# Ends of two mixers moved between the input projections, and RWKV's 32x32 products spread over the array

## The chip, the cores and the metric

The kernel runs on one core of a Trainium2 chip. Its time is the device time of one execution in microseconds; the median of three runs is given. A core has a matrix engine (TensorE, PE in the profile; its weight loads are PEld), a vector engine (VectorE, DVE), a scalar engine (ScalarE, ACT), a general one (GpSimd, POOL) and a queue from which all transfers here are issued (SyncE, SP). Each engine works through its own instructions in their order and waits on semaphores for the others. Products are made by PE into PSUM banks of 128 partitions by 512 fp32 elements.

## The reference

The kernel is a trunk of two layers over 512 latent and 256 context tokens of width 1024. Each layer is an FFN, a mixing of tokens by four groups of heads side by side, and another FFN. The mixing makes one input projection, runs GLA, a Mamba-2 (ssm), RWKV-7 and attention on its columns, puts their outputs side by side and applies one output projection:

```
ux = modulate(x, p['norm_g'][1], mx[3], mx[4]) @ p['w_in']
gla_c, gla_x = gla_mixer(...); ssm_c, ssm_x = mamba_mixer(...)
rw_c, rw_x = rwkv_mixer(...);  at_c, at_x = attention_mixer(...)
x = x + mx[5] * (concatenate([gla_x, ssm_x, rw_x, at_x]) @ p['w_out'])
```

Two of these groups have an end that needs only their own columns. That of ssm: `y = y + d_skip * xs`, times `silu(z)`, then an RMS norm over 256 columns. That of GLA: an RMS norm of each head's 64 columns, times `silu(g)`. RWKV is a recurrence over tokens, in both directions; the kernel does it in chunks of 64 tokens, for which it needs the inverse of a triangular 64x64 matrix for each head and chunk.

## The kernel before, in words

Activations lie with channels on the partitions and tokens along the free axis (768 tokens in layer 0, of which 256 are context; in layer 1 the context is needed only as a source, so many products have 512). Large products are made of three fp32r products of high and low parts (`split`, line 78, makes them: ACT rounds to the high part, DVE or POOL subtracts for the low one).

`mix` is the mixing stage. It makes the input projection in 25 tiles of 128 columns, most of them through `proj`, which loads two weight pieces, splits them and runs 24 groups of products into one of two PSUM tiles; the operand of all of them is h, eight high and eight low tiles. Between the projections stand the parts of the mixers that need them. Toward the end of `mix` come the two triangular inverses of RWKV (`x_rwkv_inverse`, lines 1410 and 1412, 31 steps of two DVE operations for each direction, its result stored in DRAM as `td` and `pd`), the gates sz0, sz1, gg1, gg0 (stored in DRAM by `spill`), the projection lg, four of attention (ak, qA, qB, av; `x_att_in`), and four of RWKV (v0, v1, r0, r1; `x_rwkv_in`, an ACT copy with scale and four DVE operations that shift by a token, lines 1221 to 1230). Only then follow

- `x_ssm_end`: multiply F by the gate z (line 1195), square on ACT, add on POOL (1202), sum over the partitions by products with a column of ones (`group_stats`), an inverse root in some dozen tiny DVE operations (`rsqrt`, lines 94 to 100), a spread of the roots back over the partitions (`spread`: ACT copy at line 838, transposes on PE at line 843), and a DVE operation that applies them (1210);
- `x_gla_end`: the same for the two tiles of GLA (lines 985 to 996);
- the fetch of gates gg1 and gg0 and their product with GLA's tiles (1843);
- `y_parts`: the high and low parts of the four tiles, written into tiles `hl0` to `hl3` and `hh4` to `hh7`, that is into the places of h.

Then `open_second` gives the rooms of the projections (SBUF and PSUM) to the second half of the stage: `rwkv`, the part of the output projection that needs GLA and ssm alone (`x_out`, PE tile `sc`, DVE line 1783, weights through one buffer `wa`), and attention (`x_att`).

`rwkv` goes through a list, `SCHEDULE`, of units (U), solves (S), steps (T) and outputs (Y); a unit is four chunks of one direction, so there are six units and six solves in each layer. `x_rwkv_unit` starts with the load of the decays (`dec`) and builds the matrices `A0`; its first products are `pr<-R,B`. `x_rwkv_solve` assembles the inverse of each 64x64 matrix from two inverted 32x32 diagonal blocks and their coupling: it loads the blocks (`PY<-pd`, `A<-td`), makes 16 products of 32x32 into one PSUM bank (`pr<-PY,A`), copies them, makes 16 more (`pr<-A,PY`) and copies these into the coupling block of `A0`. All 16 of a group read one strip of 32 partitions and write one strip of 32. `WT`, the result of the solve, has three buffers.

Program order is not engine order. The kernel is built with a planner (`schedule_with_timeline_sim=True` in the last function) that puts each engine's instructions in order ahead of time from its own estimate of durations; of what it holds for ready, the first in program order goes first. So an operation may run before others that stand ahead of it in the text. Waits and buffers follow from the tiles: a tile's place is given on when its last reader is done.

Of the kernel before, what the change touches and what calls it, by code (L numbers as in the profile page):

```python
# [12 lines left out]
ALU = mybir.AluOpType  # L13
# [39 lines left out]
class Net:  # L53
# [1363 lines left out]
    def x_rwkv_solve(self, d, b, unit, td, pd):  # L1417
        nc, rw = self.nc, self.rw
        A0, A1, ZV, ZU, R = unit
        cs = slice(4 * b, 4 * b + 4)  # L1420
        r1 = slice(64 + 32 * d, 96 + 32 * d)
        r2 = slice(96 - 32 * d, 128 - 32 * d)
        c2 = slice(32 - 32 * d, 64 - 32 * d)
        A = A0.rearrange("p h e c t -> p (h e) c t")
        P1 = rw("PY", (512,))
        for q in range(4):
            self.load(P1[r1].rearrange("p (q c t) -> p q c t", q=4, c=4)[:, q], pd[q // 2, q % 2, cs].rearrange("c s t -> s c t"))
            for i in range(2):
                self.load(A[64 + 32 * i:96 + 32 * i, q, :, 32 * i:32 * i + 32], td[i, q // 2, q % 2, cs].rearrange("c s t -> s c t"))
        py, px = self.bank(), self.bank()  # L1430
        each = [(q, c, slice(32 * (4 * q + c), 32 * (4 * q + c) + 32)) for q in range(4) for c in range(4)]
        for q, c, u in each:
            self.mm(py[r2, u], A[r1, q, c, c2], P1[r1, u])
        self.copy(P1[r2], py[r2])
        for q, c, u in each:
            self.mm(px[r1, u], P1[r2, u], A[r2, q, c, c2])
        self.copy(A.rearrange("p q c t -> p (q c) t")[r1, :, c2], px[r1].rearrange("p (q t) -> p q t", t=32))
        pw = self.bank()
        for hp in range(2):
            for c in range(4):  # L1440
                for e in range(2):
                    u = 64 * (4 * hp + c)
                    self.mm(pw[64 * e:64 * e + 64, u:u + 64], ZU[:, hp, c, e], A0[:, hp, e, c])
        WT = rw(f"WT{self.nR % self.UNITS[1]}", (2, 4, 64))
        nc.vector.tensor_copy(WT.rearrange("p h c t -> p (h c t)"), pw)
        self.heads_apart(self.bank(), lambda hp, c, e: (A0[64:128, hp, e, c], ZV[64:128, hp, c, e]), ZV)
        return WT

# [10 lines left out]

    def x_rwkv_step(self, d, n, unit, WT, PC, H, Hn):  # L1460

        nc = self.nc
        A0, A1, ZV, ZU, R = unit
        c = n % 4
        pc = self.bank("pc")
        pv = pc.rearrange("p (h x) -> p h x", h=2)
        halves = [slice(0, 64), slice(64, 128)]
        if H is not None:
            Hd = self.rw("Hd", (2, 64))
            nc.gpsimd.tensor_tensor(Hd, H, PC[:, :, n:n + 1].to_broadcast([128, 2, 64]), op=ALU.mult)  # L1470

            for hp in range(2):
                for es in halves:
                    self.mm(pv[es, hp, 0:64], WT[es, hp, c], H[es, hp])
            for e, es in enumerate(halves):
                z = ZV[64:128, :, c, e]
                nc.vector.tensor_tensor(z, pv[es, :, 0:64], z, op=ALU.add)
        for hp in range(2):
            for e, es in enumerate(halves):
                self.mm(pv[es, hp, 128:192], A1[:, hp, c, e, 1], ZV[:, hp, c, e])  # L1480
        if H is not None:
            nc.vector.tensor_tensor(Hn, Hd, pv[:, :, 128:192], op=ALU.add)
        else:
            nc.vector.tensor_copy(Hn, pv[:, :, 128:192])
        return Hn
# [42 lines left out]
    def rwkv(self, l, U, T, PC, ld, ya, need_ctx):  # L1528
# [5 lines left out]
        H = [[None], [None]]  # L1534
        unit, WT = {}, {}
        seen = set()
# [5 lines left out]
        def solve(d, s):  # L1542
            unit[d, s] = unit[d]
            WT[d, s] = self.x_rwkv_solve(d, parts[d][s], unit[d], *T[d])
        def step(d, i):
            n = self.chunks(d)[i]
            if i < 5:
                Hs[d].append(self.rw(f"H{d}{i}", (2, 64)))
            H[d].append(self.x_rwkv_step(d, n, unit[d, i // 4], WT[d, i // 4], PC[d], H[d][-1], Hs[d][i % 5]))
# [244 lines left out]
    def mix(self, l, h, need_ctx, early):  # L1794
        nc = self.nc
        nt = NT if need_ctx else NX
        self.ud = {}
        y = {}
        self.open_mix()
        self.x_rwkv_consts(l)  # L1800
        self.open_first()
        names = self.FIRST
        kp, kk, bb = [self.pair(n) for n in ("k", "kk", "bb")]
        wa = self.room("wa")
        for n, us, p in zip(names, (wa, kp[:, 0], kp[:, 1]), self.first_projs(l, names, h)):
            self.x_rwkv_in(l, n, h, NT, us, p)
        self.wa = wa
        nc.scalar.activation(out=wa[0:64], in_=wa[0:64], func=AF.Tanh)
        misc = self.x_misc(l, h)
        self.x_rwkv_prep(l, kp, kk, bb)  # L1810
        dts = self.x_ssm_dt(l, misc)
        T, PC, ld, nd = self.rwkv_inverses(l, (kk, bb))
        gqk = self.pair("gqk")
        G = [gqk[:, 0], gqk[:, 1], misc]
        self.x_gla_in(l, h, nt, G)
        self.qd, self.kn = self.pair("qd"), self.pair("kn")
        D = [self.x_gla_dir(l, d, G, nt) for d in range(2)]
        F = self.x_ssm_in(l, h, nt)
        gqk = self.pair("gqk")
        yg = [gqk[:, i] for i in range(2)]  # L1820
        for b in (2, 0, 1) if need_ctx else (0, 1):
            self.x_gla_block(l, b, D, yg)
        self.x_ssm(l, F, dts, need_ctx)
        self.x_rwkv_inverse(0, nd[0], *T[0])
        self.x_rwkv_inverse(1, nd[1], *T[1])
        for name in ("sz0", "sz1", "gg1", "gg0"):
            self.gate(l, name, h, nt)
        sg = self.x_rwkv_in(l, "lg", h, nt, self.stage())
        self.sigmoid_from(sg[:, :nt], sg[:, :nt])
        self.spill(l, "lg", sg, nt)  # L1830
        rope = self.x_att_rope()
        for name in ("ak", "qA", "qB", "av"):
            self.x_att_in(l, name, h, NT if name[0] == "a" else nt, rope)
        v, r = self.pair("kn"), self.pair("qd")
        for t, n, w in ((v, "v", NT), (r, "r", nt)):
            for hp in range(2):
                self.x_rwkv_in(l, f"{n}{hp}", h, w, t[:, hp])
        z = [self.fetch(f"sz{i}", self.gt(f"xT{i}"), nt) for i in range(2)]
        self.x_ssm_end(l, F, z, nt)
        self.x_gla_end(l, yg, nt)  # L1840
        for i in (1, 0):
            g = self.fetch(f"gg{i}", self.gt("misc"), nt)
            nc.vector.tensor_tensor(yg[i][:, :nt], g[:, :nt], yg[i][:, :nt], op=ALU.mult)
        for i in (1, 0):
            self.y_parts(y, i, yg[i], nt)
        for i in range(2):
            self.y_parts(y, 2 + i, F[i], nt)
        self.open_second()
        ya = self.hp.tile([128, 2, NT], F32, tag="hl45", name="y45")
        y[4], y[5] = ya[:, 0], ya[:, 1]  # L1850
        self.rwkv(l, (r, kp, v, kk, bb), T, PC, ld, ya, need_ctx)
        self.x_out(l, y, nt)
        self.left.close()
        self.right.close()
        self.base.close()
        self.open_early(early)
        self.x_att(l, y, need_ctx)
        self.outer.close()
        return y
# [171 lines left out]
```

## Time and profile before

| | us |
|---|---|
| median of three runs | 3250.92 |
| lowest and highest | 3242.71, 3254.85 |
| the profiled execution | 3241.78 |
| its span, first to last instruction | 3240.0 |
| PE busy | 3042.4 (94%) |
| DVE busy | 2464.2 (76%) |
| ACT busy | 1254.9 (39%) |
| POOL busy | 912.8 (28%) |

Matmuls overlap and their ends are modelled, so a busy PE is not one at its peak. The mean granted clock of PE over the span is 0.956 of full speed; it has two levels, 2.4 and 1.2 GHz. The chain that ended last is followed back from the last instruction, at each step to what released it.

### The profile page before, as it was taken

Reading aid. Unit: us, or ns where it says so; the run is one execution under the profiler, and the core shown is the slowest. Engines: PE = TensorE matmul, PEld = TensorE weight load, DVE = VectorE, ACT = ScalarE, POOL = GpSimd, SP = SyncE. Lnnn points to the kernel's source line nnn. Section 1 sums busy time; section 2 is a strip of 40 time slices with the busy share of each in tenths; the row PEclk is TensorE's granted clock in tenths of the full one; section 3 lists DMA queues with packets and bytes.
Section 4 is the critical chain, followed back from the end, with each engine's and each line's share of the span. In section 5 each row is a group of like instructions: output and inputs, shape, how many; then the busy total and the mean of one; then the engine's idle time right before and its main releaser. Section 6 shows DMA issues by size and latency. Waiting matters only on the chain.

```text
span 3240.0 us, 55398 instructions
## 1 busy us (share of the span) xinstructions
PE 3042.4 (94%) x21340; PEld 2690.3 (83%) x21340; DVE 2464.2 (76%) x4669; ACT 1254.9 (39%) x2256; POOL 912.8 (28%) x712
## 2 busy tenths in 40 slices
PE   6999999898979988999999999999898879989999
PEld 3899999777868757999998899999776767679899
DVE  7999899567854458788888787888657855487878
ACT  3333334343234444333334333333443235454444
POOL 0143333144232100233330132324145332004433
PEclk9999999898889999999999999999998879999999
DMA  6344343223224022333343233332324132133233
GB/s 253 100 132 146 124 138 117 98 73 87 77 86 120 12 95 86 101 123 118 118 130 98 72 123 105 111 120 95 115 64 120 61 93 68 43 108 101 89 102 124
DMA packets 184344, 335.79 MB, mean 104 GB/s; under 512 B 64752, under 2 KB 80976, under 8 KB 183696
## 3 DMA queue, kind: packets, MB, share of 16 engines
q1 hardware_dynamic: 184080, 332.25, 32.2%
q8 instruction: 168, 2.75, 0.4%
q14 instruction: 96, 0.79, 0.1%
HBM read 304.99 MB, written 27.18 MB: 103 GB/s over the span
## 4 chain that ended last, share of the span: by engine, by line
PE 77%; DVE 13%; DMA 5%; issue 2%; ACT 2%; SPq 1%; POOL 0%; DVEq 0%; ACTq 0%; POOLq 0%
PE pt L63 57%; PE pj L63 6%; PE pr L63 4%; PE sc L63 3%; DVE wlo L78 2%; PE pg L63 1%; DVE inv L1412 1%; DVE T L1410 1%; PE ps L63 1%; PE po L63 1%; PE pc L63 1%; SPq L60 1%; DVE t L345 1%; DMA wm<-in_w_mod 1%; DMA wraw<-in_ffn_in 1%
## 5 line engine op out<-in xcount | busy, mean ns | idle before, releaser
L77 ACT ACTIVATE whi<-wraw 128x512 fp32r<-128x512 f32 (+1 forms) x624 | 378.3, 617 | 721.8 <-PE pt L63 419.7
L63 PE MATMUL pt<-g,whi 128*128 128x512 f32 (+1 forms) x2528 | 631.9, 342 | 11.7 <-DVE X L358 4.3
L63 PE MATMUL pt<-hh,whi 128*128 128x384 f32 (+2 forms) x1664 | 533.2, 327 | 28.5 <-ACT hh L347 15.3
L63 PE MATMUL pt<-hl,whi 128*128 128x384 f32 (+2 forms) x1664 | 538.8, 325 | 4.2 <-DVE hl L348 4.2
L63 PE MATMUL pt<-hh,wlo 128*128 128x384 f32 (+2 forms) x1664 | 534.3, 324 | 0.0
L63 PEld LDWEIGHTS pt<-g,whi 128*128 128x128 f32 x2528 | 436.1, 190 | 70.0 <-DVE g L78 3.9
L78 DVE TENSOR_TENSOR wlo<-wraw,whi 128x512 fp32r<-128x512 f32 (+1 forms) x536 | 440.1, 831 | 38.3 <-ACT whi L77 37.0
L63 PE MATMUL pt<-g,wlo 128*128 128x512 f32 (+1 forms) x1264 | 422.5, 340 | 0.0
L63 PE MATMUL pt<-T,whi 128*128 128x384 f32 (+1 forms) x1728 | 406.5, 322 | 0.4 <-DVE s L544 0.4
L522 POOL TENSOR_TENSOR ws<-wraw 128x512 f32<-128x512 f32 x72 | 117.7, 1634 | 1010.1 <-DMA wraw<-in_ffn_in 749.7
L206 DVE SCALAR_TENSOR_TENSOR junk<-wm,cb 128x1024 bf16<-128x1024 f32 x272 | 357.6, 1315 | 2.9 <-DMA wm<-in_w_mod 2.7
L63 PEld LDWEIGHTS pt<-hh,whi 128*128 128x128 f32 x1664 | 317.4, 192 | 40.5 <-ACT hh L347 20.8
L63 PEld LDWEIGHTS pt<-hl,whi 128*128 128x128 f32 x1664 | 318.3, 191 | 15.4 <-DVE hl L348 6.5
L63 PEld LDWEIGHTS pt<-hh,wlo 128*128 128x128 f32 x1664 | 316.6, 191 | 8.2 <-DVE wlo L78 0.4
L358 DVE SCALAR_TENSOR_TENSOR X<-pt,hg,X 128x512 f32<-128x512 f32 (+1 forms) x376 | 224.4, 615 | 119.7 <-PE pt L63 117.4
L63 PEld LDWEIGHTS pt<-T,whi 128*128 128x128 f32 x1728 | 299.6, 188 | 1.7 <-DVE s L544 0.9
L77 ACT ACTIVATE whi<-ws 128x512 fp32r<-128x512 f32 x288 | 180.7, 629 | 292.3 <-PE pt L63 216.2
L78 DVE TENSOR_TENSOR wlo<-ws,whi 128x512 fp32r<-128x512 f32 x288 | 258.2, 899 | 28.0 <-ACT whi L77 26.7
L63 PE MATMUL pt<-T,wlo 128*128 128x384 f32 (+1 forms) x864 | 276.2, 322 | 0.0
L63 PEld LDWEIGHTS pt<-g,wlo 128*128 128x128 f32 x1264 | 239.3, 190 | 26.9 <-DVE wlo L78 0.3
L78 POOL TENSOR_TENSOR wlo<-wraw,whi 128x512 fp32r<-128x512 f32 x88 | 123.8, 1410 | 321.3 <-ACT whi L77 308.2
L63 PE MATMUL pj<-hh,whi 128*128 128x512 f32 x616 | 186.9, 370 | 13.9 <-DVE rs_r L95 7.3
(449 smaller groups left out, 5280.6 us busy)
## 6 DMA issues: line engine op xcount, KB each, us to landing
wraw<-in_ffn_in SPq DMA_DIRECT2D x176, 512.0 KB, 3.6
wm<-in_w_mod SPq DMA_DIRECT2D x144, 512.0 KB, 3.7
wraw<-in_ffn_out SPq DMA_DIRECT2D x192, 256.0 KB, 2.6
wraw<-in_w_in SPq DMA_DIRECT2D x88, 256.0 KB, 2.8
wraw<-in_w_out SPq DMA_DIRECT2D x32, 256.0 KB, 3.2
xd<-X SPq DMA_DIRECT2D x16, 384.0 KB, 2.6
wraw<-in_ffn_out SPq DMA_DIRECT2D x32, 128.0 KB, 2.0
wa<-in_w_out SPq DMA_DIRECT2D x16, 256.0 KB, 2.9
```

Of the source, the lines that this page charges most:

```text
L60: (eng or self.nc.sync).dma_start(out=dst, in_=src)
L63: self.nc.tensor.matmul(out, lhsT=lhsT, rhs=rhs, start=start, stop=stop, skip_group_check=skip)
L77: self.nc.scalar.activation(out=hi, in_=src, func=AF.Copy)
L78: (eng or self.nc.vector).tensor_tensor(lo, src, hi.bitcast(F32), op=ALU.subtract)
L206: nc.vector.scalar_tensor_tensor(out=junk, in0=w, scalar=1.0, in1=self.cb[:, s], op0=ALU.mult, op1=ALU.mult, accum_out=self.mod[l][:, s, j ...
L345: nc.vector.scalar_tensor_tensor(out=t1, in0=self.X[k][:, sg] if x is None else x, scalar=self.gs[l][:, s, 8 * n + k:8 * n + k + 1], in1=r ...
L358: self.nc.vector.scalar_tensor_tensor(out=self.X[j][:, sg], in0=o, scalar=self.hg[l][:, s, 8 * n + j:8 * n + j + 1], in1=self.X[j][:, sg], ...
L522: nc.gpsimd.tensor_tensor(w1, a21, a22, op=ALU.add)
L1410: nc.vector.tensor_tensor(tv, N[:, s, tt].unsqueeze(2).to_broadcast([96, nt, nj]), X[:, s, jj].unsqueeze(1).to_broadcast([96, nt, nj]), op ...
L1412: nc.vector.tensor_tensor(X[:, tt, jj], X[:, tt, jj], tv, op=ALU.add)
```

## The change

In `mix`, the fetch of z goes ahead of the projection lg, `x_ssm_end` behind it, `x_gla_end` behind the projection ak, and the two products with the gates behind qA and qB. In `x_rwkv_solve` the products of a group go through four heads in turn, and each head has its own strip of 32 PSUM partitions. The intermediate M and a second copy of the blocks, T2, lie compactly in the space of WT (four strips of 32 partitions, 128 elements each); T2 is loaded by four more transfers a solve. The first group's copy is one of 128x128 elements, the second's becomes four of 32x128, on ACT and DVE by turns.

```diff
         r1 = slice(64 + 32 * d, 96 + 32 * d)
-        r2 = slice(96 - 32 * d, 128 - 32 * d)
         c2 = slice(32 - 32 * d, 64 - 32 * d)
...
+        WT = rw(f"WT{self.nR % self.UNITS[1]}", (2, 4, 64))
+        T2, M = [WT[:, 0].rearrange("p a (b t) -> p (a b) t", t=32)[:, 4 * i:4 * i + 4] for i in range(2)]
         for q in range(4):
+            self.load(T2[32 * q:32 * q + 32], td[1 - d, q // 2, q % 2, cs].rearrange("c s t -> s c t"))
             self.load(P1[r1].rearrange("p (q c t) -> p q c t", q=4, c=4)[:, q], pd[q // 2, q % 2, cs].rearrange("c s t -> s c t"))
...
-        each = [(q, c, slice(32 * (4 * q + c), 32 * (4 * q + c) + 32)) for q in range(4) for c in range(4)]
-        for q, c, u in each:
-            self.mm(py[r2, u], A[r1, q, c, c2], P1[r1, u])
-        self.copy(P1[r2], py[r2])
-        for q, c, u in each:
-            self.mm(px[r1, u], P1[r2, u], A[r2, q, c, c2])
-        self.copy(A.rearrange("p q c t -> p (q c) t")[r1, :, c2], px[r1].rearrange("p (q t) -> p q t", t=32))
+        each = [(q, c, slice(32 * q, 32 * q + 32), slice(32 * c, 32 * c + 32)) for c in range(4) for q in range(4)]
+        for q, c, qs, u in each:
+            self.mm(py[qs, u], A[r1, q, c, c2], P1[r1, 128 * q + 32 * c:128 * q + 32 * c + 32])
+        self.copy(M, py[:, :128].rearrange("p (c t) -> p c t", c=4))
+        for q, c, qs, u in each:
+            self.mm(px[qs, u], M[qs, c], T2[qs, c])
+        for q in range(4):
+            self.copy(A[r1, q, :, c2], px[32 * q:32 * q + 32, :128].rearrange("p (c t) -> p c t", c=4), q % 2)
...
-        WT = rw(f"WT{self.nR % self.UNITS[1]}", (2, 4, 64))
...
             self.gate(l, name, h, nt)
+        z = [self.fetch(f"sz{i}", self.gt(f"xT{i}"), nt) for i in range(2)]
+
         sg = self.x_rwkv_in(l, "lg", h, nt, self.stage())
...
         self.spill(l, "lg", sg, nt)
+        self.x_ssm_end(l, F, z, nt)
         rope = self.x_att_rope()
         for name in ("ak", "qA", "qB", "av"):
             self.x_att_in(l, name, h, NT if name[0] == "a" else nt, rope)
+            if name == "ak":
+                self.x_gla_end(l, yg, nt)
+            elif name[0] == "q":
+                i = 1 if name == "qA" else 0
+                g = self.fetch(f"gg{i}", self.gt("misc"), nt)
+                nc.vector.tensor_tensor(yg[i][:, :nt], g[:, :nt], yg[i][:, :nt], op=ALU.mult)
         v, r = self.pair("kn"), self.pair("qd")
...
-        z = [self.fetch(f"sz{i}", self.gt(f"xT{i}"), nt) for i in range(2)]
-        self.x_ssm_end(l, F, z, nt)
-        self.x_gla_end(l, yg, nt)
-        for i in (1, 0):
-            g = self.fetch(f"gg{i}", self.gt("misc"), nt)
-            nc.vector.tensor_tensor(yg[i][:, :nt], g[:, :nt], yg[i][:, :nt], op=ALU.mult)
```

## Rows read from the trace of the kernel before

**Rows 1.** The page: busy time (us, share, instructions), and the chain by engine.
```profile
PE 3042.4 (94%) x21340; PEld 2690.3 (83%) x21340; DVE 2464.2 (76%) x4669; ACT 1254.9 (39%) x2256; POOL 912.8 (28%) x712
...
PE 77%; DVE 13%; DMA 5%; issue 2%; ACT 2%; SPq 1%; POOL 0%; DVEq 0%; ACTq 0%; POOLq 0%
```
**Rows 2.** Stretches: length, PE, PEld, DVE, ACT, POOL busy, clock, DMA, GB/s.
```profile
938.40:961.40 23.00, 8.64 (x52) 7.35 (x50) 19.88 (x53) 11.70 (x16) 7.26 (x8) 0.62 0.31 91
961.40:1135.00 173.60, 170.65 (x2195) 137.36 (x2195) 87.39 (x199) 74.75 (x125) 39.56 (x46) 0.94 0.24 67
...
2560.00:2600.00 40.00, 27.31 (x185) 23.07 (x184) 37.79 (x118) 7.74 (x13) 14.65 (x11) 0.74 0.15 51
2619.40:2635.50 16.10, 2.95 (x17) 2.42 (x15) 12.07 (x30) 7.79 (x13) 7.55 (x8) 0.62 0.40 119
2635.50:2800.00 164.50, 161.00 (x2007) 126.24 (x2007) 82.53 (x188) 74.12 (x123) 39.08 (x46) 0.91 0.20 56
2657.30:2674.40 17.10, 16.77 (x118) 13.77 (x119) 3.91 (x9) 3.90 (x7) 3.82 (x4) 0.50 0.26 80
```
**Rows 3.** Timeline of PE, layer 0: start, us, operation, count [idle <-releaser].
```profile
912.71 0.82 PE L843 MATMUL pg<-cst,spr 128*128 128x128 f32 x6
...
938.37 0.72 PE L63 MATMUL ps<-cst,cb 128*128 128x1 f32 x6
938.95 2.82 PE L63 MATMUL pg<-cst,sq 128*128 128x2 f32 x24
946.88 1.54 PE L843 MATMUL ps<-cst,spr 128*128 128x128 f32 x6 [5.10 <-ACT spr L838]
...
960.47 1.01 PE L63 MATMUL sc<-yp,woh 128*128 128x512 f32 x2 [8.28 <-ACT yp L77]
961.41 3.43 PE L63 MATMUL pr<-R,B 64*128 64x128 f32 x24
```
**Rows 4.** Timeline of DVE in layer 0, the last split of GLA's tiles.
```profile
960.67 0.94 DVE L78 TENSOR_TENSOR yp<-gqk,yp 128x768 fp32r<-128x768 f32 x1
```
**Rows 5.** Timeline of PE in layer 1, around its last projection.
```profile
2612.60 0.60 PE L843 MATMUL ps<-cst,spr 128*128 128x128 f32 x4
...
2619.43 0.95 PE L63 MATMUL pg<-cst,sq 128*128 128x2 f32 x8
2628.74 1.97 PE L843 MATMUL pg<-cst,spr 128*128 128x128 f32 x8 [8.36 <-ACT spr L838]
2635.54 3.67 PE L63 MATMUL pr<-R,B 64*128 64x64 f32 x24 [4.84 <-DVE B L1357]
```
**Rows 6.** Timeline of ACT in layer 1, the split of ssm's tiles.
```profile
2615.99 1.32 ACT L77 ACTIVATE yp<-F 128x512 fp32r<-128x512 f32 x2 [2.50 <-PE pj L63]
```
**Rows 7.** Timeline of DVE in layer 0, one operation of a root.
```profile
889.88 1.86 DVE L98 TENSOR_TENSOR rs_t<-rs_r,rs_h 128x12 f32<-128x12 f32 x1
```
**Rows 8.** Waits from 2500 to 2640 us: who for whom, us, times, longest.
```profile
PE pj L63 <- DVE rs_r L95: 7.3, 1, 7.3
```
**Rows 9.** Instructions on tile PY: ns min/median/max, first and last start, forms.
```profile
L63 PE MATMUL pr<-PY,A x384: 191/191/212, 980.1 to 2775.1; 32*32 32x32 f32 x192
...
L815 ACT ACTIVATE PY<-pr x12: 588/590/593, 981.4 to 2775.3; 32x512 f32<-32x512 f32 x12
```
**Rows 10.** Timeline of PE around one group of 32x32 products, layer 0.
```profile
1085.51 1.19 PE L63 MATMUL pr<-PY,A 32*32 32x32 f32 x32
1086.63 1.12 PE L63 MATMUL po<-gS,V 128*128 128x512 f32 x2
```
**Rows 11.** Timeline of PE: products of GLA, 64 rows by 32 columns.
```profile
708.66 0.44 PE L63 MATMUL pg<-vT,kt 64*32 64x64 f32 x28
```
**Rows 12.** Timeline of PE: one step of RWKV, two diagonal 64x64 corners.
```profile
1002.52 0.45 PE L63 MATMUL pc<-H,WT 64*64 64x64 f32 x8
```
**Rows 13.** Instructions of line 815, ACT copies: the smallest from PSUM in 128 partitions.
```profile
L815 ACT ACTIVATE gqk<-pg x10: 367/384/385, 785.1 to 2524.1; 128x256 f32<-128x256 f32 x10
```
**Rows 14.** Timeline of SP: the four loads of P1 in one solve.
```profile
952.25 1.77 SPq L60 DMA_DIRECT2D PY<-pd  x4
```

## The prediction

> **What bounds the kernel now.** I read the page first: its busy times and the chain that ended last [rows 1]. TensorE (PE) is busy 94% of the span and holds 77% of the chain, VectorE (DVE) 13%. So a change pays where PE stands still, or where its own instructions get shorter. Next the busy times by stretch, around the two mixing stages (layer 0 from about 600 to 1200 us, layer 1 from about 2300 to 2850 us) [rows 2]. From the last input projection to the first RWKV product PE is busy 8.64 of 23.0 us in layer 0 and 2.95 of 16.1 us in layer 1: 14.4 and 13.1 us idle, at a granted clock of 0.62, a mixture of the two levels 1.2 and 2.4 GHz. Behind them PE is full: 170.65 of 173.6 us and 161.0 of 164.5 us.
>
> What PE does in the first hole [rows 3]: the sums of both ends (938.37, 938.95) stand behind the last projection; then it waits for DVE and ScalarE (ACT), does transposes for the spreads (the first at 946.88; three such rows up to 952.2), and waits until 960.47. The wait is for the last operand of the output projection, split only when the gate has been multiplied in; DVE does the last split at 960.67 [rows 4]. In layer 1 the planner has already put the sums of ssm between the projections; the sums of gla follow at 2619.43, its transposes at 2628.74 after 8.4 us of idle, the first RWKV product at 2635.54 after 4.8 [rows 5]. The change aims at these holes and at the 32x32 products behind them.
>
> **Part 1, the ends between the projections.** Nothing is removed: squares, sums, roots, spreads and gate products (lines 1195 to 1211, 985 to 997, 1843) get an earlier place in program order, and so do the fetches of z and of the two gates on the SP queue. Their PE work goes into the projections unshortened except by the clock: the six instructions of three transposes take 1.54 us at 946.88 and 0.82 us at 912.71, where the granted clock was full [rows 3]. Three such rows in layer 0 and 1.97 us of transposes in layer 1 make about 2 us of gain in layer 0 and 1 in layer 1; the operations behind the hole that also ran at the half level I take at 1 us in layer 1.
>
> What is late next, when the ends are done? The splits stay behind the projections: their high and low parts are written into tiles of h, which the last projection still reads. The split of F in layer 1 shows it: 1.32 us for two, released by PE's last projection products [rows 6]. So the output projection can start some 1 to 3 us after the last projection, not at once, and then its own weights (one buffer) limit it. I leave 3 us idle per layer. The first RWKV unit needs the decays, and in layer 0 also r, whose shift is four DVE operations; I expect it some 6 us behind the last projection, with the output projection under it.
>
> Against this stand new waits inside the projections. Each end puts two pieces on PE's ordered queue, sums and transposes, and each waits for DVE or ACT; all later projections queue behind it, and behind these the loads and splits of their weights. DVE is the crowded engine there: 37.79 of 40 us busy between 2560 and 2600 [rows 2], since the triangular inverse runs on it, and one of the root's tiny operations took 1.86 us [rows 7]. One wait in this stretch is already 7.3 us long [rows 8]. Bounds for the added waits: nothing (the planner finds a slot in which the operand is there) to 4 pieces of 7.3 us a layer. I take 3 us in layer 0, where DVE has room after 896 us, and 5 us in layer 1: near the lower end, as only the gla end and part of the ssm end are new to these queues.
>
> Layer 0: -14.4 - 2 + 3 + 3 = about -10 us (bounds -16 and +18). Layer 1: -13.1 - 2 + 3 + 5 = about -7 us (bounds -15 and +17).
>
> **Part 2, the 32x32 products.** There are twelve solves (six a layer), each with two groups of 16 products, 32 PE instructions, since an fp32 product is two: 384 of the first kind in both layers [rows 9]. A group takes 1.19 us, 1.00 from first start to last and 0.19 for the last to run out, and the next PE operation starts just as it ends [rows 10]: the 16 products stand in one 32x32 corner of the array, one behind the other at 32 ns. After the change, consecutive products go to four different column strips (first group) or four diagonal corners (second). The trace has a relative: products of 64 rows by 32 columns that walk over four column strips and two row halves. 28 of them take 0.44 us [rows 11], so start to start about (0.44 - 0.22)/27 = 8 ns. By it a new group takes 32 x 8 = 0.25, plus 0.19, 0.45 us: 0.74 less, and 24 x 0.74 = 18 us if PE is the bound at each. That PE is 98% busy there speaks for nearly all of it; that this includes tails and that the solve's chain also has copies in it speaks for less. I take three quarters, -13 us (bounds 0 and -18).
>
> One rule speaks against the relative. The Trainium skill, TensorE: Matmul & The Clock Gate, section "Wait — 56ns, not 53.3ns?", says that matmuls never start closer than about 25 ns, however small. By it a group would take 32 x 25 = 0.80 and 0.19 us, and part 2 would give 24 x 0.2 = 5 us (an estimate from that page). The 8 ns just read from the trace disagree with it.
>
> The second group also writes one bank from four row strips at a time. The nearest row: the step's products of H and WT go through two diagonal 64x64 corners into one bank, 8 in 0.45 us [rows 12]: (0.45 - 0.22)/7 = 33 ns for 64 columns, half of what twice 32 ns would be in a queue. So the corners overlap. The Trainium skill, TensorEngine Tiling (Array Packing), "Gotcha 1: PSUM Pressure", says that different row tiles cannot access one bank at the same time. By it the second group would keep its 1.19 us and part 2 give half, 9 us at most: 4 us less than I take, inside the forecast's own range. The row disagrees.
>
> Copies. The first group's copy goes from 32x512 (0.59 us [rows 9]) to 128x128 elements; the nearest ACT copy is 128x256 at 0.384 us [rows 13], so I say 0.3. The second, also 0.59 us, becomes four copies of 32x128, two on ACT and two on DVE, about 0.5 us on two queues. Gain 0.2 to 0.3 us a solve where PE waits for it: -2 us in twelve (bounds +2 and -5).
>
> Transfers. Each solve loads T2 as well: 4 more issues of 32x128 on SP, which as the neighbouring four took 1.77 us together [rows 14]; 48 in all, 21 us of SP. SP is 1% of the chain [rows 1]; the cover is that T2 needs no product of its unit, only a free WT slot, so it can be loaded ahead. T2 now waits for the steps three units back, and behind it on SP stand P1, the A blocks, and the output projection's weights; those steps are long done in program order. In return the second group no longer waits for the A blocks. I cost all this at 0 (bounds -5, the waits for A blocks, and +8, if four tenths of the 21 us stand ahead of a weight that PE waits for).
>
> **Sum.** -10 - 7 - 13 - 2 = -32 us on the profiled execution, 3241.78 us (span 3240.0). The three timed runs have a median of 3250.92, 9 us above it; the same difference gives 3219 us.
>
> **Rivals.**
> Quarters don't overlap: each group stays at 1.19 us, as instructions are fed at 32 ns whatever the corner. For it: the 32 ns of rows 10, which could be a feed rate; against it rows 11 and 12. Then only part 1 and the copies are left, -19: 3232. Chance 0.14. (The skill's 25 ns would land at 3227.)
>
> The RWKV chain is the limit: PE fills the holes with the output projection, but the chain of steps starts only some 7 us earlier in each layer, and the end of the stage follows it. For it: the first RWKV product comes behind decays and r, not behind the ends. Against: PE is 98% busy behind, so filler done early shortens it. -14 and a third of part 2, -4: 3233. Chance 0.18.
>
> The clock gives more: behind the hole of layer 1 stands another stretch of 17.1 us at half clock, PE busy 16.77 [rows 2], just after a pair of 32x32 groups. At the full clock its work would take about half; if that and its like in layer 0 vanish, some 6 us each come on top: 3207. Chance 0.10.
>
> Slower: the pieces of the ends block PE's ordered queue. If the planner places sums and transposes earlier than DVE delivers, eight pieces wait, as the one of rows 8. From an average of 5 us each (40 in all, against the 8 in my sum) all 32 us are gone; at 6 us the result is 3219 + 40 = 3259. For it: DVE's 37.79 of 40 us. Against: after 896 us in layer 0 DVE is mostly idle. Chance 0.10.
>
> **How the numbers follow.** Forecast 0.48 (its own range 3205 to 3233), then 0.14, 0.18, 0.10, 0.10. One run in ten falls below 3195, one in ten above 3250: range 3193 to 3250. What this measurement can tell from no change is 0.5%, 16 us, so faster means under 3234.7: nearly all of the forecast, the clock case, most of the quarters' case and half of the chain's: 0.72. Slower means over 3267: 0.08. Same: 0.20.
>
> **What would show it.** Right: the two holes under 5 us of PE idle, with the output projection's products right behind the last projection; groups of 32 in about 0.45 us; sums of both ends among the projections. Wrong: PE idle before the sums or transposes between 885 and 945 or between 2560 and 2620 us that adds up to over 15 us a layer; groups still over 1 us; or PE idle returning behind 1130 us, where the steps end.

## The result, and the profile after

The changed kernel takes 3285.78 us (median of 4 runs, 3277.07 to 3288.78) against 3252.44 beside it: a ratio of 1.0100 with a 95% interval of 1.0081 to 1.0119. That is 33 us slower; 3219 was forecast, and 3250 was the end of the range. The profiled executions differ by 44 us (span 3284.1 against 3240.0), because the one of before was 11 us under its median.

The page, busy times and the chain by engine, against [rows 1]:

```profile
PE 3079.1 (94%) x21340; PEld 2710.8 (83%) x21340; DVE 2479.0 (75%) x4693; ACT 1249.7 (38%) x2268; POOL 910.8 (28%) x712
...
PE 78%; DVE 12%; DMA 5%; issue 2%; ACT 2%; SPq 1%; POOL 0%; DVEq 0%; ACTq 0%; POOLq 0%
```

PE issues the same 21340 products and is busy 37 us longer; its idle time grew by 7. So the loss is mostly work that takes longer, not waiting. In which stage? Stretches of the kernel before: first each layer's mixing stage from the first input projection to the end of RWKV, then the half-clock stretch around each hole, then RWKV of layer 1 from its first 32x32 group (length, busy time of PE, PEld, DVE, ACT and POOL, clock, DMA share, GB/s):

```profile
577.30:1172.60 595.30, 542.18 (x5045) 439.94 (x5045) 373.24 (x887) 222.20 (x356) 170.80 (x162) 0.91 0.24 71
2297.40:2828.30 530.90, 475.74 (x4303) 372.54 (x4303) 336.58 (x810) 211.04 (x342) 169.33 (x158) 0.89 0.25 72
...
943.80:964.30 20.50, 8.17 (x41) 6.96 (x42) 17.74 (x46) 9.49 (x14) 9.27 (x8) 0.50 0.33 99
2623.20:2643.70 20.50, 10.12 (x43) 8.52 (x43) 12.86 (x29) 7.00 (x12) 9.16 (x9) 0.50 0.31 93
2653.90:2828.30 174.40, 168.08 (x2056) 126.83 (x2055) 89.09 (x217) 77.56 (x131) 32.13 (x41) 0.94 0.19 52
```

The same of the changed kernel: both stages; then hole and RWKV of layer 0 and of layer 1, as in [rows 2]; the longest half-clock stretch behind the holes; RWKV of layer 1 from its first group:

```profile
575.60:1190.80 615.20, 556.57 (x5046) 447.08 (x5047) 384.18 (x899) 220.94 (x365) 172.06 (x162) 0.89 0.24 70
2317.40:2871.70 554.30, 495.74 (x4312) 383.75 (x4312) 342.72 (x825) 211.38 (x352) 169.05 (x158) 0.86 0.24 69
...
954.90:964.90 10.00, 1.33 (x5) 0.83 (x4) 9.81 (x17) 6.03 (x9) 7.24 (x7) 0.68 0.48 127
964.90:1138.50 173.60, 167.29 (x2058) 132.41 (x2058) 83.61 (x190) 68.83 (x126) 38.17 (x42) 0.88 0.24 69
2648.20:2660.60 12.40, 5.65 (x17) 3.56 (x16) 10.13 (x16) 6.65 (x12) 9.60 (x10) 0.77 0.54 169
2660.60:2825.10 164.50, 156.43 (x1819) 119.82 (x1819) 77.23 (x177) 67.68 (x123) 36.89 (x41) 0.82 0.23 60
2685.70:2709.60 23.90, 23.68 (x127) 18.06 (x128) 5.20 (x11) 5.65 (x11) 5.11 (x5) 0.50 0.33 106
...
2682.00:2871.70 189.70, 174.72 (x2043) 128.47 (x2042) 94.36 (x233) 76.94 (x140) 30.16 (x39) 0.86 0.15 39
```

The two mixing stages took 19.9 and 23.4 us more, nearly all of the 44. They hold as many products as before (5046 for 5045, 4312 for 4303), PE is busy 14.4 and 20.0 us longer in them, and the clock fell from 0.91 to 0.89 and from 0.89 to 0.86. Before, each hole carried 20.5 us at half clock, with PE busy only 8.17 and 10.12 us of them: half speed cost little there. Now the holes are short, and the longest half-clock stretch behind them follows the first solve of layer 1, with PE busy 23.68 of 23.9 us.

For the whole span I added up, from the trace's clock record and PE's rows, PE's busy time at the lower level (1.2 GHz): 228 us before, 306 after. Half of the difference is lost, 39 us; idle time adds 7.5, and the work itself, counted at full clock, shrank by 2.5. So 39 of the 44 us between these two executions are clock. Most of it lies behind the first RWKV product, where PE's busy time at the lower level rose from 19 to 48 us in layer 0 and from 28 to 59 in layer 1; in the projections it rose from 65 to 73 and from 66 to 75. The timed runs bear it out with less: the mean clock was 0.9525 over 114 runs of before and 0.9452 over the 4 of after, and among executions of one same kernel 0.001 of mean clock goes with 2.0 us (a line through all 279 timed runs, each kernel with its own level). By that line about 15 us of the 33 go with the clock.

### The profile page after: what moved, and what is told of

Same layout as the page of the kernel before. It is cut to its first block, busy times and chain, and to the rows that moved or that the text cites. A ratio compares the mean times of both kernels' runs of the same rounds, so it can differ in the third digit from the quotient of the medians.

```text
span 3284.1 us, 55527 instructions
## 1 busy us (share of the span) xinstructions
PE 3079.1 (94%) x21340; PEld 2710.8 (83%) x21340; DVE 2479.0 (75%) x4693; ACT 1249.7 (38%) x2268; POOL 910.8 (28%) x712
## 4 chain that ended last, share of the span: by engine, by line
PE 78%; DVE 12%; DMA 5%; issue 2%; ACT 2%; SPq 1%; POOL 0%; DVEq 0%; ACTq 0%; POOLq 0%
PE pt L63 56%; PE pj L63 7%; PE pr L63 5%; PE sc L63 3%; PE pg L63 2%; DVE wlo L78 2%; PE ps L63 2%; PE po L63 1%; DVE T L1410 1%; PE pc L63 1%; SPq L60 1%; DVE inv L1412 1%; DVE t L345 1%; DMA wraw<-in_ffn_in 1%; DMA wm<-in_w_mod 1%
## 5 line engine op out<-in xcount | busy, mean ns | idle before, releaser
L63 PE MATMUL pt<-g,whi 128*128 128x512 f32 (+1 forms) x2528 | 633.1, 342 | 13.7 <-DVE X L358 6.6
L78 DVE TENSOR_TENSOR wlo<-wraw,whi 128x512 fp32r<-128x512 f32 (+1 forms) x536 | 438.4, 828 | 45.1 <-ACT whi L77 43.7
L63 PEld LDWEIGHTS pt<-hl,whi 128*128 128x128 f32 x1664 | 318.2, 191 | 17.1 <-DVE hl L348 7.8
```

Of the source, the lines that this page charges most:

```text
L63: self.nc.tensor.matmul(out, lhsT=lhsT, rhs=rhs, start=start, stop=stop, skip_group_check=skip)
L78: (eng or self.nc.vector).tensor_tensor(lo, src, hi.bitcast(F32), op=ALU.subtract)
```

## The experiments

Medians are of the timed runs, ratios against the kernel before on the same chip with their 95% intervals, clocks the mean over the timed runs. Two theories stand against each other at first: P, that the moved pieces of the ends block PE's ordered queue, so that PE waits; and C, that PE does more of its work at the lower clock.

**The change in parts.** e1 takes the hunks in `mix` alone, e2 those of `x_rwkv_solve` alone, e4 only the two lines of `mix` on ssm; e3 is the changed kernel with the heads outermost, so that four products in a row hit one quarter. The edits of e4 (to the kernel before) and of e3 (to the changed one):

```diff
+        z = [self.fetch(f"sz{i}", self.gt(f"xT{i}"), nt) for i in range(2)]
         sg = self.x_rwkv_in(l, "lg", h, nt, self.stage())
...
+        self.x_ssm_end(l, F, z, nt)
         rope = self.x_att_rope()
...
-        z = [self.fetch(f"sz{i}", self.gt(f"xT{i}"), nt) for i in range(2)]
-        self.x_ssm_end(l, F, z, nt)
         self.x_gla_end(l, yg, nt)
```

```diff
-        each = [(q, c, slice(32 * q, 32 * q + 32), slice(32 * c, 32 * c + 32)) for c in range(4) for q in range(4)]
+        each = [(q, c, slice(32 * q, 32 * q + 32), slice(32 * c, 32 * c + 32)) for q in range(4) for c in range(4)]
```

> The kernel before with part 1 alone (ends of ssm and GLA between the projections; solves as before). Theory C (the clock): the time lost sits behind the solves, where PE stands at half clock 28 us longer in layer 0 and 33 us longer in layer 1 than before, so without the new solves the stretches behind the projections go back to some 211 and 193 us and the total lies near before: 3245 to 3265 us. Theory P (the pieces of the ends block PE's queue): the projections end 18 and 10 us later and nothing pays it back: 3270 to 3285 us.

> The kernel before with part 2 alone (products on four quarters, compact states, T2; ends as before). Theory C: groups take 0.45 us, PE waits for the copies between them instead, and the half-clock stretches behind solves grow from 2 to 4 or 5 of 14 to 24 us: 3260 to 3285 us. Theory P: part 2 is what was forecast of it, some 10 to 15 us less than before: 3237 to 3245 us.

> The changed kernel whose 16 products of a group go through the heads one after the other (head outermost), so that four in a row hit the same quarter; states, loads and copies as changed. Theory C: a group takes about 1.2 us again, PE is less idle behind a solve, the clock falls less often, and the time is no longer than the changed kernel's, perhaps 10 to 15 us less: 3270 to 3288 us. Theory P: the products cost their 18 us again on top of the changed kernel: about 3300 us.

> The kernel before with the fetch of z and the end of ssm alone moved between the projections; the end of GLA and its gates as before. Theory C: little changes behind the projections; the hole after the last projection stays, since GLA's chain still stands there: 3245 to 3260 us. Theory P: half of the added waits of the projections: about 3268 us.

Measured: e1 3269.93 us, 1.0052 (1.0027 to 1.0076), clock 0.950. e2 3262.30, 1.0019 (0.9999 to 1.0039), 0.9465. e3 3282.70, 1.0095 (1.0069 to 1.0122), 0.948. e4 3250.99, 0.9997 (0.9974 to 1.0019), 0.954. e2, e3 and e4 lie in C's ranges; e1 lies between the two, at the edge of P's. Part 1 loses 17 us, and as ssm's end alone (e4) loses nothing, it must be gla's end with the gates, or both ends together. Part 2 gains nothing where 13 us were forecast; its interval holds 1, at a clock 0.006 lower. In e3 the groups took 0.9 us, twice those of the changed kernel (C had expected 1.2), at no cost in time that these runs can tell. And the stretches of e1: its mixing stages, then two of the half-clock stretches in RWKV of layer 1:

```profile
576.80:1174.40 597.60, 548.64 (x5039) 445.01 (x5039) 374.46 (x886) 221.57 (x355) 171.27 (x162) 0.90 0.24 71
2304.20:2859.90 555.70, 503.69 (x4303) 397.65 (x4302) 337.38 (x810) 209.96 (x342) 168.38 (x158) 0.84 0.23 69
...
2704.60:2721.70 17.10, 17.02 (x143) 14.52 (x144) 8.72 (x21) 3.66 (x8) 0.94 (x1) 0.50 0.12 33
2728.50:2749.00 20.50, 19.82 (x165) 16.91 (x166) 8.10 (x20) 4.14 (x7) 1.75 (x3) 0.50 0.08 19
```

Layer 1 has exactly the 4303 products of before and is 28 us busier with them, at 0.84 instead of 0.89. PE's idle time in the projections rose by only 1.8 and 1.4 us: theory P has its blocked pieces, but they are small. Added up as above, PE's busy time at the lower level is 304 us in e1 against 228: 38 us lost, more than the 28 by which its span is longer.

**The copies.** A solve of the changed kernel (1102 to 1110 us) shows the second loss, PE first:

```profile
1102.03 0.45 PE L63 MATMUL pr<-PY,A 32*32 32x32 f32 x32
...
1104.16 0.45 PE L63 MATMUL pr<-WT 32*32 32x32 f32 x32
...
1106.69 0.33 PE L63 MATMUL pr<-A,ZU 128*64 128x64 f32 x2
1106.95 0.32 PE L63 MATMUL pr<-ZV,A 64*64 64x64 f32 x2
1107.20 0.68 PE L63 MATMUL pr<-A,ZU 128*64 128x64 f32 x14
1107.81 0.33 PE L63 MATMUL pr<-ZV,A 64*64 64x64 f32 x4
1108.08 0.33 PE L63 MATMUL pr<-A,ZU 128*64 128x64 f32 x2
1108.33 0.44 PE L63 MATMUL pr<-ZV,A 64*64 64x64 f32 x6
1108.70 0.68 PE L63 MATMUL pr<-A,ZU 128*64 128x64 f32 x14
1109.31 0.80 PE L63 MATMUL pr<-ZV,A 64*64 64x64 f32 x20
```

ACT and then DVE in the same solve:

```profile
1105.27 0.27 ACT L815 ACTIVATE A<-pr 32x128 f32<-32x128 f32 x1
1105.88 0.27 ACT L815 ACTIVATE A<-pr 32x128 f32<-32x128 f32 x1 [0.35 <-DVE A L813]
```

```profile
1105.57 0.29 DVE L813 COPY A<-pr 32x128 f32<-32x128 f32 x1 [0.32 <-ACT A L815]
...
1106.66 0.29 DVE L813 COPY A<-pr 32x128 f32<-32x128 f32 x1
```

The kernel before, the same products in its fifth solve:

```profile
1092.35 1.15 PE L63 MATMUL pr<-A,ZU 128*64 128x64 f32 x32
1093.43 1.15 PE L63 MATMUL pr<-ZV,A 64*64 64x64 f32 x32
```

The groups take 0.45 us, as forecast. But the four copies take turns: each starts when the one before has ended on the other engine (1105.27, 1105.57, 1105.88), and the last stands behind other DVE work until 1106.66: 1.7 us from first to last, where one copy took 0.59 [rows 9]. And since each copy releases the products of one head, the planner put the 64 products behind them (`pr<-A,ZU` and `pr<-ZV,A`) in eight pieces: 3.4 us instead of 2.2. Theory K holds that the chain of copies is what costs, theory S that it is the split. Three repairs of the changed kernel:

```diff
 f2_whole: the product that needs the fourth copy first, the others queued behind it
...
+        product(1, 0, 1)
+        with self.tc.issue_after(self.told(mybir.EngineType.PE)):
...
 f5_act: all four copies on ACT
-            self.copy(A[r1, q, :, c2], px[32 * q:32 * q + 32, :128].rearrange("p (c t) -> p c t", c=4), q % 2)
+            self.copy(A[r1, q, :, c2], px[32 * q:32 * q + 32, :128].rearrange("p (c t) -> p c t", c=4), 0)
 f7_two_banks: heads 0 and 2 in one bank, 1 and 3 in another
...
-            self.mm(px[qs, u], M[qs, c], T2[qs, c])
+            self.mm(px[q % 2][qs, u], M[qs, c], T2[qs, c])
...
```

> The changed kernel, with the products behind the four second copies held together: the first of the 32 products of a solve needs the fourth copy, and the other 31 are queued behind it. In the changed kernel each copy releases the products of its own head, and PE goes through them in seven or eight runs of 2 to 20 (pr<-A,ZU and pr<-ZV,A together 48 us in both mixing phases against 29 us before, start to start). Theory S (the release by heads splits the products, and the alternation of the two kinds costs): the two kinds go back to two runs of 32 and to 30 to 35 us together; 12 x 1.1 us = 13 us less than the changed kernel, 3272, if the fourth copy is no new wait. Theory K (the chain of the copies, 1.7 us from the first start to the last end, is the cost, not the split): products whole, but PE now waits for the end of the chain: 3286 or a few us more. Theory C (the granted clock sets the time: across executions of all kernels so far 0.001 of mean clock is 2.1 us, and the changed kernel has 0.945 against 0.953): no change beyond 5 us unless the clock moves.

> The changed kernel, with all four second copies on ACT. In the changed kernel they alternate ACT, DVE, ACT, DVE and each starts when the one before has ended, on the other engine (1.7 us from the first start to the last end in the solve at 1105.27 us). Theory K (the chain with its hops costs): four in a row on one engine take 4 x 0.27 = about 1.1 us, and none stands behind other DVE work; 0.6 us less in each of 12 solves, about -7 us, 3279. Theory S (the split by heads): products still split, within 3 us of 3286. Theory C: within 5 us of 3286 at the same mean clock.

> The changed kernel, with the second group's output in two banks, heads 0 and 2 in one (copied by ACT), heads 1 and 3 in the other (copied by DVE); one more of the three rotating banks is taken in each solve. Theory K: if the alternation comes from the shared bank, the two engines now copy side by side, 2 x 0.28 = 0.56 us instead of 1.7; up to 1.1 us less in each of 12 solves, -13 us, 3273, less what the scarcer banks cost (bounds 0 to +10). If the alternation has another cause, the copies go on taking turns. Theory S: products still split into pieces, within 4 us of 3286. Theory C: within 5 us at the same mean clock.

Measured: f2 3277.58 us, 1.0075 (1.0055 to 1.0095), clock 0.945. f5 3279.79, 1.0077 (1.0060 to 1.0093), 0.947. f7 3276.91, 1.0076 (1.0062 to 1.0090), 0.945. Copies of f7 in one solve, ACT and then DVE, and the products behind them on PE:

```profile
1107.38 0.56 ACT L815 ACTIVATE A<-pr 32x128 f32<-32x128 f32 x2
```

```profile
1107.12 0.61 DVE L813 COPY A<-pr 32x128 f32<-32x128 f32 x2 [0.68 <-PE pr L63]
```

```profile
1109.56 1.15 PE L63 MATMUL pr<-A,ZU 128*64 128x64 f32 x32
1110.64 1.03 PE L63 MATMUL pr<-ZV,A 64*64 64x64 f32 x28
```

With two banks the engines copy side by side, and all four are done in 0.8 us: the shared bank made the chain. Each repair gives 6 to 9 us at about the same clock, about a quarter of the loss. Their intervals overlap that of the changed kernel, so no single gain is clear of noise; all three point the same way. f5 came out at K's time, f2 6 us above S's, f7 4 us above K's; C's 5 us are passed by 1 to 4. The products behind the copies took 30.2 us before in 25 pieces and 50.4 us in 79 pieces in the changed kernel (PE's starts, added up over both stages). They take 33.0 us in 24 pieces in f2, 43.7 in 66 in f5, and 43.2 in 46 in f7. So each repair shortens them, f2 by far the most and without gaining more time: these runs do not tell K from S. The repairs of f2 and f7 at once were run in the changed kernel only with the added work below (h3).

**The clock, first attempt.** Behind the moved ends the output projection's large products ran out earlier (81 and 67 us behind the last input projection, where it had been 90 and 73); f6 holds half of them back:

```diff
...
-                piece(j, s)
+                if j < 4:
+                    piece(j, s)
+                else:
+                    with self.tc.issue_after(self.solved[3]):
+                        piece(j, s)
```

> The changed kernel, with pieces 4 to 7 of the output projection's eight column groups held on PE until the fourth of the six solves of the layer is through (nothing else changed). In all profiles so far the large products of the output projection run out some 70 to 90 us behind the last input projection, and most stretches at half clock of the mixing phase stand behind that (before: 100.9 us behind in layer 0; with both parts 88.9, 119.7 in layer 0, 37.5, 75.0, 98.9 in layer 1). Theory C (the clock falls where only the RWKV step's small products are left, and the ends' move brings the large ones ahead): half-clock time of both phases falls from 109 us to about 50, mean clock back to 0.953, and 15 us go: 3270; if the hold leaves holes ahead of the fourth solve, part of it is eaten (bound +15). Theories S and K: the copies and the splits stay, so at equal clock nothing changes; holding filler back costs 5 to 15 us: 3290 to 3300.

Measured: 3314.29 us, 1.0193 (1.0177 to 1.0209), clock 0.939. A miss of all theories. Two half-clock stretches of f6 in layer 1, in the time without those products:

```profile
2688.70:2709.20 20.50, 18.17 (x152) 15.97 (x152) 6.74 (x16) 5.36 (x10) 3.22 (x4) 0.50 0.30 90
2712.50:2726.20 13.70, 13.61 (x131) 11.80 (x124) 4.47 (x13) 1.71 (x4) 1.34 (x2) 0.50 0.06 10
```

In this layer the half clock went where the large products were missing (35 to 103 us behind the last projection), and while they ran (111 to 134 us) the clock was full. So they seem to matter, but holding them back only moves the loss. Their lack is not the whole cause either: the longest half-clock stretch behind the changed kernel's holes, from 2685.7, fell while they ran.

**The clock, by added work.** 96 products of 128x512 that nobody needs, four behind each 32x32 group; the real ones overwrite them. Behind the first group:

```diff
...
+        with self.tc.issue_after(self.told(mybir.EngineType.PE)):
+            for n in range(4):
+                self.mm(px, self.extra[:, :128], self.extra[:, :512])
...
```

g1 adds them to the changed kernel. g2 is e2 with f2's and f7's repairs, g3 is g2 with the end of ssm moved, g4 is g3 with the added products.

> The changed kernel with work added: in each solve four unneeded 128x512 products (y against itself, overwritten by the real ones) behind the first 32x32 group and four behind the second, where PE waits for the copies; 96 in all at about 0.22 us, 21 us of PE. In the changed kernel each half-clock stretch of the mixing phases begins 3 to 6 us behind a solve. Theory C (the clock falls because the solve leaves PE with only small products and waits; split by profile, 39 of the 44 us between the two profiled executions are work done at half clock): the half-clock stretches behind the solves get fewer, the mean clock rises from 0.945 to 0.950 or more, and the time is not above 3286, down to 3265. Theories S and K (waits and splits at the copies): the clock is a bystander, the added 21 us show in the time where PE is the bound: 3295 to 3307.

> The kernel before with the products on quarters (no end moved), with both repairs of the copies: the second group's output in two banks, and the products behind it held together. Theories S and K: the quarters alone were 3262 (3246 at equal clock); with both repairs up to 13 us less at the same clock of 0.9465: about 3250, and 3240 if the clock is that of before. Theory C: what the solve saves comes back as half clock: within 5 us of 3257, mean clock at or below 0.947.

> As the last (quarters, two banks, products held together), and the end of ssm with the fetches of z moved between the projections, the end of gla and the gates where they were before. The end of ssm alone was 3251 at a clock of 0.954. Theories S and K: the gains add, 3250 - 1: 3245 to 3252. Theory C: the clock decides; 3250 to 3262 at 0.946 to 0.949.

> As the last, with eight unneeded 128x512 products in each solve as in the run with the changed kernel (21 us of PE added). Theory C: the mean clock rises by 0.004 or more against the last one, and the time is equal or lower: 3235 to 3250. Theories S and K: up to 21 us slower than the last: 3262 to 3272.

Measured: g1 3266.25 us, 1.0051 (1.0034 to 1.0067), clock 0.953. g2 3257.00, 1.0025 (1.0013 to 1.0037), 0.948. g3 3253.41, 1.0007 (0.9995 to 1.0019), 0.948. g4 3243.65, 0.9984 (0.9969 to 1.0000), 0.9565. RWKV of layer 1 in g1, from its first group, to be held against 2682.00:2871.70 above:

```profile
2673.50:2852.20 178.70, 171.82 (x2127) 125.89 (x2126) 94.06 (x232) 78.91 (x143) 34.69 (x43) 1.00 0.20 51
```

PE issues 84 more products in this stretch, 48 of them the added ones, and is busy 2.9 us less: the clock is 1.00 instead of 0.86. In the profiled executions the gain is all in layer 1, whose stage is 22 us shorter than in the changed kernel; that of layer 0 is 5 us longer. Twenty-one us of useless work took 20 us off the changed kernel (16 by the ratios), and 10 off g3 (8). Theories S and K asked for 3295 or more in g1 and 3262 or more in g4; this is the clock. In g1 the products behind the copies also come in fewer pieces, 56 instead of 79, so a part of its gain may be theirs; in g3 and g4 they are whole (25 and 24 pieces), and the gain there has no such rival. g2 and g3, without added work, lie in C's ranges of time, g3 only 1 us above that of S and K.

Controls: h1 has the same products in the kernel before, h2 in e1; h3 is the changed kernel with both repairs and the products; h4 is g4 with sixteen a solve.

> The kernel before with eight unneeded 128x512 products in each of its solves (four behind each 32x32 group, 21 us of PE). Theory C as it stands (the quarters are what lost the clock behind the solves): before loses little there (20 and 29 us of half clock in its two mixing phases), so at most 10 us come back for 21 added: 3255 to 3270, slower than before, clock 0.955 to 0.958. Rival W (any mixing phase of this kernel gains from such products, the change has nothing to do with it): 3235 to 3248, as fast as the best so far.

> The ends moved, old solves, with the same eight products in each solve. The ends alone were 3270 at clock 0.950, with 24 and 78 us of half clock in the mixing phases of the profile. Theory C1 (the ends' loss is half clock behind the solves too): clock 0.955 or more, 3250 to 3262. Theory C2 (it sits in the projections, where the pieces of the ends now make PE wait): clock at 0.952 or less, 3272 to 3290.

> The changed kernel with both repairs of the copies (two banks, products held together) and the eight products in each solve: the 3244 kernel with the end of gla and the gates moved too. If the move of gla's end is neutral once the clock behind the solves is kept up: 3240 to 3250. If it has a cost of its own in the projections: 3252 to 3262, and its clock is then lower by 0.002 or more.

> The 3244 kernel (quarters, both repairs, the end of ssm moved, eight unneeded products in each solve) with sixteen. 21 us of PE more. Theory C: the phases have only 31 and 16 us of half clock left, so at most some 15 us can come back: 3245 to 3265. Rival W: faster again, below 3240.

Measured: h1 3257.00 us, 1.0004 (0.9989 to 1.0019), clock 0.9585. h2 3263.38, 1.0023 (1.0003 to 1.0043), 0.956. h3 3247.46, 0.9980 (0.9964 to 0.9997), 0.957. h4 3262.01, 1.0023 (1.0007 to 1.0039), 0.957. In before the added work comes back almost whole too, 17 to 20 us of the 21, where theory C had allowed 10 at most: the kernel before loses clock in this way as well. But it gains nothing, so W falls. With the added work in both, the changed kernel is 9 us slower than the kernel before (g1 against h1; 15 by the ratios) instead of 33: the clock, with the fewer pieces, explains 18 to 24 us. With both repairs too (h3 against h1) it is 8 to 10 us faster. In e1 the added work gains some 7 us and lifts the clock as C1 said, to a time just above C1's range (C2 asked for a clock of 0.952 or less). With repairs and clock, gla's move costs nothing that these runs can tell (h3 against g4). Sixteen are too many: the clock is no higher than with eight, and the work is paid.

Half as many, two behind each group: i1 in g4, i2 in h3.

> The 3244 kernel with four unneeded products in each solve (two behind each group), not eight: 10.5 us of PE less. If four hold the clock (0.955 or more): 3232 to 3242. If the clock answers to the sum of the work, half of what eight brought (0.948 to 0.9565) is lost: 0.952, and 3244 to 3252.

> The changed kernel with both repairs and four unneeded products in each solve. If four hold the clock: 3235 to 3244, at 0.955 or more. If not: 3250 to 3262, at 0.951 or less.

Measured: i1 3262.98 us, 1.0025 (1.0012 to 1.0038), clock 0.953. i2 3247.46, 0.9979 (0.9963 to 0.9994), 0.9555. i1 lies above both of its ranges, i2 between its two. They disagree on whether four hold the clock, so that stays open, and with it whether gla's move gains. The best versions (g4, h3, i2) are 5 to 8 us under before: intervals at or just below 1, and less than the 0.5% that counts as no change here.

## Why the prediction was wrong

The clock terms of part 1 failed first: "about 2 us of gain in layer 0 and 1 in layer 1", and everything else priced as if the clock elsewhere stayed, a cost put at nothing without a reason. The rival "the clock gives more" had the right place and the wrong sign. The 17.1 us at half clock behind the hole of layer 1 [rows 2] became three stretches of 23.9, 13.7 and 13.7 us, each behind a solve, and the loss is about 15 of 33 us by the line through the timed runs, 18 to 24 by g1 against h1, 39 of 44 by the profiled pair. It comes from both parts: e1's clock is 0.003 lower, e2's 0.006. That the clock sets the time, g4 against g3 shows by experiment; why it falls behind these solves stays open. Ahead of the longest of the three stretches PE waited for no copy of the solve. PE and ACT there:

```profile
2685.92 1.22 PE L63 MATMUL sc<-yp,woh 128*128 128x512 f32 x2 [2.41 <-ACT woh L77]
```

```profile
2685.24 0.63 ACT L77 ACTIVATE woh<-wa 128x512 fp32r<-128x512 f32 x1 [2.42 <-DMA wa<-in_w_out]
```

PE waited for the split of one of the output projection's weights, and ACT for its transfer; the solve's copies stood behind that on ACT, until 2685.89.

"Copies": -2 with bounds of +2 and -5 came out with the wrong sign. The row it was sized by [rows 13] was right for one copy (0.27 us); "about 0.5 us on two queues" for the four was not, since they share a bank and took 1.7, and the splitting of the products behind was not thought of. Repaired, 6 to 9 us come back, which is above the upper bound, but not clear of noise run by run.

"I leave 3 us idle per layer": measured 8.7 and 6.7, from the rows of the holes above. So the holes gave up 12 us of idle time where 21 were forecast, and 14 us of idle time came back behind the first RWKV product, which the sum left out. What is late next is seen on PE of the changed kernel, at the hole of layer 0:

```profile
954.45 0.51 PE L63 MATMUL pj<-hh,wlo 128*128 128x512 f32 x2
958.11 1.27 PE L63 MATMUL sc<-yp,woh 128*128 128x512 f32 x4 [3.15 <-ACT woh L77]
964.99 1.40 PE L63 MATMUL pr<-R,B 64*128 64x128 f32 x9 [5.60 <-DVE B L1357]
```

The split of the output projection's weights comes late (3.15 us), and the first unit's operand B costs 5.60, a wait that the prediction had put under the output projection.

"Part 2, -13" was right as PE work and wrong as time. The two groups went from 14.4 and 16.4 us to 5.1 and 10.0 in both stages of the changed kernel (PE's starts, added up), 15.7 less. But e2 is no faster than before: its clock is 0.006 lower, and the products behind the copies took 13.9 us more, by the split and by the clock. The 8 ns of [rows 11] held.

"Transfers", costed at 0, was not tested by itself. ACT's waits for the transfers of the output projection's weights between 2600 and 2900 us rose from 3.0 us to 18.1. They are 14.9 in e1, which has no T2, and 6.4 in e2, which has it: most of this came with the moved ends, as "its own weights (one buffer) limit it" had said, and not with the loads of T2.

The slower rival (blocked pieces of the ends) has its waits in layer 1 of the changed kernel:

```profile
2617.97 0.98 PE L63 MATMUL pj<-hh,whi 128*128 128x512 f32 x2 [6.27 <-DVE kn L1230]
...
2634.15 0.76 PE L63 MATMUL pj<-hh,whi 128*128 128x512 f32 x1 [4.50 <-DVE rs_t L99]
```

But 7.3 us of such a wait stood there before [rows 8], and PE's idle time in the projections rose by 6 and 1 us: it was no more than a small part, near the 8 us of the sum. The projections are 18.0 and 8.5 us longer, but mostly with PE busy, with the moved products and at the lower clock. (The upper bound of layer 0 in the sum is -14.4 - 2 + 3 + 29.2, so +16 and not +18; nothing hangs on it.)

## What to carry to other kernels

Where PE is full, price an edit in work at the granted clock: the half clock in the holes here was cheap, because PE was idle for half of it or more, and once they were closed the half-clock time stood in full stretches. Read the clock of the stretches behind the edit, not only of the edited one; a quick test is to add large unneeded products at the place, in the kernel before too, and see whether the time falls. When one copy is cut into several, look at what each reads: here the pieces of one bank on two engines took turns, and each released its own part of what waited behind.

## What the runs showed of the hardware

Thirty-two 32x32 instructions over four quarters take 0.45 us, also where four row strips write one bank; in e3, with four in a row in a quarter, about 0.9; one corner alone 1.19 [rows 10]. The unexpected one: 96 added products of 128x512 in the solves raise the mean clock of the whole execution from 0.945 to 0.953, and the same 96 raise it in the kernel before from 0.9525 to 0.9585. In the RWKV stage of the changed kernel five half-clock stretches begin 1.6 to 5.2 us behind the first 32x32 group of a solve, where PE does small products with short waits between them, for copies, for operands of attention and once for a weight; seven of the twelve solves have none behind them. The longest in its mixing stages (41.0 us from 791.3, 37.5 from 2521.9) stand in the projections, where no solve is, and no run here tested what brings them. Half the added work gave 0.953 in one kernel and 0.9555 in the other, and sixteen a solve gave no more than eight.
